# Row normalisation: the first tile's chunks in another partition order, and its last scale on VectorE

## The chip, the cores and the metric

The kernel runs on one core of a Trainium2 chip. The metric is the time of one execution on the device in microseconds, the median of several runs. Three runs of the kernel before took 82.49, 82.53 and 82.61 us, with a median of 82.53 us.

## The reference

The input is a matrix `x` of 1024 rows and 4096 columns in float32. Each row is divided by its Euclidean norm:

```python
norm = np.sqrt(np.sum(x ** 2, axis=-1, keepdims=True) + eps)   # eps = 1e-12
return (x / norm).astype(np.float32)
```

16.78 MB are read and 16.78 MB are written. A row's result depends on that row alone.

## The kernel before

**Tiles.** A tile holds 128 partitions with R = 4 whole rows each, 512 rows or 8.4 MB. There are two tiles (`n_tiles = 1024 / 512`), and each has its own buffer, so neither waits for the other's buffer. Four neighbouring rows are one contiguous run of 4 x 4096 x 4 B = 64 KiB in the input; such a run is called a chunk here. In the view `x_t` (L176) partition p of tile t holds chunk p of that tile, and `out_t` (L177) is the same view of the output.

**Transfers.** All four big transfers are issued from SyncE (SP) and travel on one queue: the load of tile 0, the load of tile 1 (both L192), the store of tile 0, the store of tile 1 (both L213). `first_load_to_front` moves the first load to the very beginning of the program, in front of the start-up barrier. A store is issued when its whole tile has been scaled, and moves the whole tile. `one_barrier_behind_last_store` arranges the end of the program so that it waits for the stores once.

**Calculation, for each tile.** The engines run their instructions in the order of the program, and the order in the loop at L197 to L213 is written by hand. A tile has four row groups, r = 0 to 3: row group r is the r-th row of every partition, 128 x 4096 elements.

- `square_act` (L33): ScalarE squares a row group and accumulates the sum of each row. Groups 0, 1 and 2 go this way.
- `square_dve` (L42): VectorE does the same for group 3, at the start of the tile.
- `norm`: a square root on ScalarE (L53), then a reciprocal on VectorE (L59), each over one number in every partition.
- `scale` (L64): VectorE multiplies a row group in place by its reciprocals. `scale_act` (L69) does the same on ScalarE.

The scales of groups 0, 1 and 3 are on VectorE in both tiles. The last one, of group 2, is on ScalarE in the first tile and on VectorE in the second:

```python
if i < n_tiles - 1:
    g.scale_act(2)
else:
    g.scale(2)
store = nc.sync.dma_start(out=out_t[i], in_=g.flat())
```

Semaphores are placed by the framework from the data that each instruction reads and writes. `Square`, `Sqrt` and the copy with a scale are activation functions of ScalarE. L184 sets the constant eps, and L231 is the program's frame.

Of the kernel before, what the change touches and what calls it, by code (L numbers as in the profile page):

```python
# [8 lines left out]
ACT_F = mybir.ActivationFunctionType  # L9
# [4 lines left out]
class RowGroups:  # L14
# [48 lines left out]
    def scale(self, r):  # L63
        self.nc.vector.tensor_scalar_mul(  # L64
            out=self.x[:, r], in0=self.x[:, r], scalar1=self.rstd[:, r : r + 1]
        )

    def scale_act(self, r):
        self.nc.scalar.activation(  # L69
            out=self.x[:, r],  # L70
            in_=self.x[:, r],
            func=ACT_F.Copy,
            scale=self.rstd[:, r : r + 1],
        )


def first_load_to_front(nc, load):

    def move(program):
        blocks = program.main_func.blocks
        entry = blocks[0].instructions
        if any(i.name == load.name for i in entry):
            return
        body = next(
            b.instructions  # L90
            for b in blocks
            if any(i.name == load.name for i in b.instructions)
        )
        at = next(n for n, i in enumerate(body) if i.name == load.name)
        assert not body[at].sync_info.on_wait
        before = next(
            n
            for n, i in enumerate(entry)
            if i.engine == mybir.EngineType.SP and isinstance(i, mybir.InstDrain)
        )  # L100
        entry.insert(before, body.pop(at))

    nc.at_finalize(move)


def one_barrier_behind_last_store(nc, store):

    SP, POOL = mybir.EngineType.SP, mybir.EngineType.Pool

    def waits(i):
        return i.sync_info.on_wait if i.sync_info is not None else []

    def move(program):
        sem = store.sync_info.on_update[0].id
        tail = program.main_func.blocks[-1].instructions  # L120

        def take(which):
            at = next(n for n, i in enumerate(tail) if which(i))
            return tail.pop(at)

        def place(instructions, which):
            at = max(n for n, i in enumerate(tail) if which(i))
            tail[at:at] = instructions

        arrivals = [  # L130
            n
            for n, i in enumerate(tail)
            if i.engine == SP and isinstance(i, mybir.InstDrain)
        ]
        if any(w.id == sem for w in waits(tail[arrivals[-2]])):
            return
        everything = take(
            lambda i: i.engine == SP and any(w.id == sem for w in waits(i))
        )
        place([everything], lambda i: i.engine == SP and isinstance(i, mybir.InstDrain))  # L140
        reset = take(
            lambda i: i.engine == POOL
            and isinstance(i, mybir.InstDrain)
            and i.is_reset_sema
        )
        clear = take(lambda i: i.engine == POOL and isinstance(i, mybir.InstISA))
        place(
            [reset, clear],
            lambda i: i.engine == POOL and isinstance(i, mybir.InstEventSemaphore),
        )  # L150

    nc.at_finalize(move)


@with_exitstack
def kernel(
    ctx: ExitStack,
    tc: tile.TileContext,
    x: bass.AP,
    axis: bass.AP,  # L160
    eps: bass.AP,
    out: bass.AP,
):
    nc = tc.nc
    P = nc.NUM_PARTITIONS

    assert isinstance(axis, int) and axis in (-1, len(x.shape) - 1)
    eps = float(eps)

    x = x.flatten_outer_dims()  # L170
    out_flat = out.flatten_outer_dims()
    N, D = x.shape
    R = 4
    assert N % (P * R) == 0
    n_tiles = N // (P * R)
    x_t = x.rearrange("(t p r) d -> t p (r d)", p=P, r=R)  # L176
    out_t = out_flat.rearrange("(t p r) d -> t p (r d)", p=P, r=R)  # L177

    io = ctx.enter_context(tc.tile_pool(name="io", bufs=n_tiles))
    scratch_pool = ctx.enter_context(tc.tile_pool(name="scratch", bufs=1))  # L180
    stats = ctx.enter_context(tc.tile_pool(name="stats", bufs=n_tiles))

    eps_t = scratch_pool.tile([P, 1], F32)
    nc.vector.memset(eps_t, eps)  # L184
    sq_act = scratch_pool.tile([P, D], F32)
    sq_dve = scratch_pool.tile([P, D], F32)
    scratch = {"act": sq_act, "dve": sq_dve}

    groups = []
    for i in range(n_tiles):  # L190
        g = RowGroups(nc, io, stats, scratch, D, R, eps_t)
        load = nc.sync.dma_start(out=g.flat(), in_=x_t[i])  # L192
        if i == 0:
            first_load_to_front(nc, load.ins)
        groups.append(g)

    for i, g in enumerate(groups):  # L197
        g.square_dve(R - 1)
        g.square_act(0)
        g.norm(0)  # L200
        g.scale(0)
        g.square_act(1)
        g.norm(1)
        g.norm(R - 1)
        g.scale(1)
        g.scale(R - 1)
        g.square_act(2)
        g.norm(2)
        if i < n_tiles - 1:
            g.scale_act(2)  # L210
        else:
            g.scale(2)
        store = nc.sync.dma_start(out=out_t[i], in_=g.flat())  # L213
    one_barrier_behind_last_store(nc, store.ins)


# [33 lines left out]
```

## Time and profile before

| What | Value |
|---|---|
| median of three runs | 82.53 us |
| the profiled execution: its time | 82.49 us |
| the profiled execution: its span | 80.7 us |
| VectorE busy | 26.2 us (33% of the span) |
| ScalarE busy | 30.1 us (37%) |
| DMA queue: bytes, packets' share of 16 engines | 33.55 MB, 97.0% |
| loads issued (SP) | 0.0 and 0.8 us |
| first instruction on tile 0, on tile 1 | 21.89 us, 41.25 us |
| stores issued (SP) | 39.2 and 56.6 us |
| one scale on VectorE (L64), on ScalarE (L69) | 2.353 us, 3.708 us |

The times in the profile count from the start of the span; what lies between the span and the execution's time is start and end of the program outside it. SPq is the queue of instructions of SyncE, which issues the transfers. In lists of groups and waits, the name left of an arrow waited for the name right of it, and the numbers give the sum, the count and the longest wait. In the chain of waits each line has a start, a length and the work that the later work had to wait for. In a table of stretches each line has a stretch of the span, its length, the busy time of VectorE, ScalarE and GpSimd with the number of their instructions, the clock that TensorE was granted (it does nothing here), the share of the 16 DMA engines that was busy, and the rate in GB/s; a transfer's packet counts where it starts. 512 of the 576 packets carry 64 KiB each, and 64 carry the 4 bytes that tell of a landing.

### The profile page before, as it was taken

The page shows a single profiled execution, that of the slowest core. Times are in us where ns is not written, and L with a number is a line of the kernel's source. Part 1 is how long each engine was busy: PE and PEld are TensorE (multiplying, and loading weights), DVE is VectorE, ACT ScalarE, POOL GpSimd, SP SyncE. Part 2 cuts the span into 40 slices and gives each one's busy share as a digit, 9 for nine tenths or more (in the row PEclk, how much of TensorE's full clock was granted, in tenths as well). Part 3 has the DMA queues.
Part 4 walks back from the last instruction along what each step waited for, and adds up shares of the span by engine and source line. Part 5 has one row for each costly group of instructions (what it writes and reads, how often), then busy time and mean ns, then how long its engine had stood idle before and what let it go on. Part 6 is the DMA issues. An engine that isn't in the chain of part 4 may idle for free.

```text
span 80.7 us, 93 instructions
## 1 busy us (share of the span) xinstructions
DVE 26.2 (33%) x20; ACT 30.1 (37%) x23; POOL 0.2 (0%) x4
## 2 busy tenths in 40 slices
DVE  0000000000199599920059986999000000000000
ACT  6000000000199999989459999930000000000000
POOL 0000000000000000000000000000000000000000
DMA  9099998299998299998399992999993999993990
GB/s 520 0 520 520 520 520 390 130 520 520 520 520 390 130 520 520 520 520 390 130 520 520 520 520 130 390 520 520 520 520 130 390 520 520 520 520 130 390 520 0
DMA packets 576, 33.55 MB, mean 416 GB/s; under 512 B 64, under 2 KB 64, under 8 KB 64
## 3 DMA queue, kind: packets, MB, share of 16 engines
q1 hardware_dynamic: 576, 33.55, 97.0%
HBM read 16.78 MB, written 16.78 MB: 416 GB/s over the span
## 4 chain that ended last, share of the span: by engine, by line
DMA 50%; ACT 10%; DVE 9%; issue 0%
DMA xt<-in_x_dram 50%; ACT sq_act L33 9%; DVE xt L64 9%; ACT rstd L53 1%; DVE rstd L59 0%
## 5 line engine op out<-in xcount | busy, mean ns | idle before, releaser
L33 ACT ACTIVATE sq_act<-xt 128x4096 f32<-128x4096 f32 x6 | 21.6, 3608 | 21.9 <-DMA xt<-in_x_dram 21.9
L42 DVE SCALAR_TENSOR_TENSOR sq_dve<-xt 128x4096 f32<-128x4096 f32 x2 | 8.8, 4425 | 26.8 <-DMA xt<-in_x_dram 26.8
L64 DVE TENSOR_SCALAR xt<-xt,rstd 128x4096 f32<-128x4096 f32 x7 | 16.5, 2353 | 0.2
L69 ACT ACTIVATE xt<-xt,rstd 128x4096 f32<-128x4096 f32 x1 | 3.7, 3708 | 0.2 <-DVE rstd L59 0.2
L53 ACT ACTIVATE rstd<-ssq,eps_t 128x1 f32<-128x1 f32 x8 | 2.1, 288 | 0.1
L59 DVE RECIPROCAL rstd<-rstd 128x1 f32<-128x1 f32 x8 | 1.3, 159 | 2.4 <-ACT rstd L53 2.4
L33 ACT ACT_TABLE_LOAD x1 | 1.3, 1283 | 0.8 <-PEq L231 0.8
L53 ACT ACT_TABLE_LOAD x1 | 1.3, 1283 | 0.0
L33 ACT ACTIVATION_READ_ACCUMULATOR sq_act<-xt 128x1 f32 x6 | 1.1, 185 | 0.0
L184 DVE MEMSET eps_t<- 128x1 f32 x1 | 0.1, 59 | 0.9 <-PEq L231 0.9
L42 DVE DVE_READ_ACCUMULATOR sq_dve<-xt 128x1 f32 x2 | 0.2, 82 | 0.0
L231 POOL MEMSET const-bfloat16-1.0<- 128x1 bf16 x1 | 0.1, 101 | 0.0
L231 POOL MEMSET const-uint8-127<- 128x1 uint8 x1 | 0.1, 101 | 0.0
L231 POOL MEMSET const-float32-0.0<- 128x1 f32 x1 | 0.1, 98 | 0.2 <-issue 0.2
L231 POOL MEMSET const-float32-1.0<- 128x1 f32 x1 | 0.1, 98 | 0.0
## 6 DMA issues: line engine op xcount, KB each, us to landing
xt<-in_x_dram SPq DMA_DIRECT2D x2, 31.2
out_dram<-xt SPq DMA_DIRECT2D x2, 22.6
```

The lines of the kernel that those rows point to most:

```text
L33: self.nc.scalar.activation(out=sq_a, in_=self.x[:, r], func=ACT_F.Square, accum_out=self.ssq[:, r : r + 1],)
L42: self.nc.vector.scalar_tensor_tensor(out=sq_v, in0=self.x[:, r], scalar=1.0, in1=self.x[:, r], op0=ALU.mult, op1=ALU.mult, accum_out=self ...
L53: self.nc.scalar.activation(out=self.rstd[:, r : r + n], in_=self.ssq[:, r : r + n], func=ACT_F.Sqrt, bias=self.eps_t,)
L59: self.nc.vector.reciprocal(out=self.rstd[:, r : r + n], in_=self.rstd[:, r : r + n])
L64: self.nc.vector.tensor_scalar_mul(out=self.x[:, r], in0=self.x[:, r], scalar1=self.rstd[:, r : r + 1])
L69: self.nc.scalar.activation(out=self.x[:, r], in_=self.x[:, r], func=ACT_F.Copy, scale=self.rstd[:, r : r + 1],)
L184: nc.vector.memset(eps_t, eps)
L231: nc = _bacc.Bacc("TRN2", target_bir_lowering=False, num_devices=1)
```

## The change

There are two edits.

1. `scale_act` is removed, and the last scale of the first tile is `scale(2)` on VectorE, as in the second tile.
2. The first tile is loaded and stored through another view. The 128 chunks of the tile are numbered 32b + g, with b = 0 to 3 and g = 0 to 31, and partition 4g + b holds chunk 32b + g. The first partitions of neighbouring groups of four (partitions 0, 4, 8, ...) hold neighbouring chunks 0, 1, 2, ..., and the four partitions of one group hold chunks that are 32 chunks apart, 2 MiB. The second tile keeps the plain view. The view in memory has three dimensions, 32 x 4 x 16384 elements; on chip the tile is 128 x 16384 as before.

```diff
-    def scale_act(self, r):
-        self.nc.scalar.activation(
-            out=self.x[:, r],
-            in_=self.x[:, r],
-            func=ACT_F.Copy,
-            scale=self.rstd[:, r : r + 1],
         )
...
+    B = 4
+    x_f = x.rearrange("(t b g r) d -> t g b (r d)", b=B, g=P // B, r=R)
+    out_f = out_flat.rearrange("(t b g r) d -> t g b (r d)", b=B, g=P // B, r=R)
+    x_v = [x_f[0]] + [x_t[i] for i in range(1, n_tiles)]
+    out_v = [out_f[0]] + [out_t[i] for i in range(1, n_tiles)]
...
-        load = nc.sync.dma_start(out=g.flat(), in_=x_t[i])
+        load = nc.sync.dma_start(out=g.flat(), in_=x_v[i])
...
-        if i < n_tiles - 1:
-            g.scale_act(2)
-        else:
-            g.scale(2)
-        store = nc.sync.dma_start(out=out_t[i], in_=g.flat())
+        g.scale(2)
+        store = nc.sync.dma_start(out=out_v[i], in_=g.flat())
```

More of the change, by code (lines that the diff above doesn't have):

```diff
@@ L65, in scale @@
             out=self.x[:, r], in0=self.x[:, r], scalar1=self.rstd[:, r : r + 1]
-        )
-    def scale_act(self, r):
-        self.nc.scalar.activation(
-            out=self.x[:, r],
-            in_=self.x[:, r],
-            func=ACT_F.Copy,
-            scale=self.rstd[:, r : r + 1],
         )
```

## The prediction

> **What bounds the kernel now.** I read the page first, then the queue's waits, the chain in order of time, the instructions around the first store, and last a table of stretches cut where the transfers change hands.
>
> The page: span, traffic per slice, the one queue.
>
> ```profile
> span 80.7 us, 93 instructions
> DVE 26.2 (33%) x20; ACT 30.1 (37%) x23; POOL 0.2 (0%) x4
> DMA  9099998299998299998399992999993999993990
> DMA packets 576, 33.55 MB, mean 416 GB/s; under 512 B 64, under 2 KB 64, under 8 KB 64
> q1 hardware_dynamic: 576, 33.55, 97.0%
> ```
>
> Both compute engines work a third of the span; the one DMA queue carries 33.55 MB with its packets covering 97.0% of 16 engines' time. The dips in the digits are an artefact: a packet is 64 KiB and counts in the slice where it starts. So the limit is the transfers, in the order load 0, load 1, store 0, store 1.
>
> The queue's own waits, and the chain in order of time (start, length, what):
>
> ```profile
> SPq L245 <- DMA out_dram<-xt: 22.7, 2, 19.3
> SPq L213 <- ACT xt L69: 17.3, 1, 17.3
> ```
>
> ```profile
> 0.79 40.44 DMA xt<-in_x_dram
> 41.23 0.02 issue
> 41.25 3.72 ACT sq_act L33 x2
> ...
> 54.23 2.35 DVE xt L64
> ```
>
> The chain stops at the last calculation, 54.23 + 2.35 = 56.58 us. It doesn't set the end: behind it the program waits 19.3 us in one piece for stores. Store 1 is issued at 56.6 and joins a queue that is busy with store 0 until about 60.4.
>
> The instructions around the first store (start, length, engine, line):
>
> ```profile
> 34.95 0.29 ACT L53 ACTIVATE rstd<-ssq,eps_t 128x1 f32<-128x1 f32 x1
> 35.28 0.16 DVE L59 RECIPROCAL rstd<-rstd 128x1 f32<-128x1 f32 x1 [0.56 <-ACT rstd L53]
> 35.48 3.71 ACT L69 ACTIVATE xt<-xt,rstd 128x4096 f32<-128x4096 f32 x1 [0.23 <-DVE rstd L59]
> 39.21 0.35 SPq L213 DMA_DIRECT2D out_dram<-xt  x1
> 41.25 3.62 ACT L33 ACTIVATE sq_act<-xt 128x4096 f32<-128x4096 f32 x1 [2.06 <-DMA xt<-in_x_dram]
> 41.25 4.43 DVE L42 SCALAR_TENSOR_TENSOR sq_dve<-xt 128x4096 f32<-128x4096 f32 x1 [5.81 <-DMA xt<-in_x_dram]
> ```
>
> Store 0 is issued at 39.21, when ScalarE's 3.71 us scale ends, before load 1 has landed (41.25). VectorE stands idle for 5.81 us there.
>
> The stretches (start:end, length, VectorE, ScalarE, GpSimd busy, clock, DMA share, GB/s):
>
> ```profile
> 1.00:4.05 3.05, 0.00 (x0) 1.07 (x1) 0.00 (x0) 1.00 1.04 344
> 4.05:20.95 16.90, 0.00 (x0) 0.00 (x0) 0.00 (x0) 1.00 1.00 434
> 20.95:40.30 19.35, 11.96 (x9) 16.97 (x12) 0.00 (x0) 1.00 1.00 434
> 40.30:40.52 0.22, 0.00 (x0) 0.00 (x0) 0.00 (x0) 1.00 0.01 0
> 40.52:59.90 19.38, 14.23 (x10) 11.87 (x10) 0.00 (x0) 1.00 1.00 433
> ```
>
> The queue moves 32 rows of 16 packets. In rows 2 to 16 a packet takes 2.418 us by the packet records (65,536 B x 16 / 2.418 us = 434 GB/s, as in the table). The first row alone is slow: 3.16 us in the mean (2.51 to 3.52). Load 0 hands over to load 1, and store 0 to store 1, with no gap. Load 1 hands over to store 0 with a hole: its last packets end between 40.33 and 40.92, and the first store packets begin between 40.53 and 41.02, in the mean 0.18 us later. The row behind the hole takes 2.454 us a packet instead of 2.42.
>
> **The change, part by part.**
>
> *The last scale of tile 0 goes from ScalarE to VectorE.* Removed: one ACT instruction of 3.71 us (L69). Added: one VectorE scale (L64), 2.353 us by the seven in the trace. Both wait for the reciprocal that ends at 35.44. VectorE has nothing else until 41.25, so the added 2.35 us lie in the 5.81 us of idle time and would cost something only if tile 1 landed before 37.8. ScalarE has its next work at 41.25 too, so its 3.71 us bring nothing by themselves. Nothing is queued between this scale and tile 1 on either engine. No table load is involved: the two in the trace belong to L33 and L53, which stay.
>
> What moves is store 0's issue on SP's queue: 39.21 - (3.71 - 2.35) = about 37.85. SP has nothing in front of it, and behind it waits only store 1, at 56.6. The transfer can't begin before load 1 is through its rings at 40.33 to 40.92, so the 1.36 us are not 1.36 us of gain. The question is the 0.18 us hole. Load 0 shows 1.02 us from issue to first packet; store 0's first packet comes 1.32 us after its issue (40.53 - 39.21), hence just as the rings run dry. Issued at 37.85 it would be ready by about 39.2 on the same 1.32 us, at least 1.1 us before the first ring is free. The two handovers whose successor was issued well ahead (0.79 for 21.0, 56.6 for 60.0) show a hole of 0.00. They are the nearest rows, so I take the hole as closing: 0.18 us, and with it the slow row behind it, 2.454 - 2.42 = 0.03. Together -0.21 us. Other end: both of those handovers keep the direction, and this is the only one in which reading HBM turns into writing it; if the hole is the price of turning, the gain is 0.00.
>
> *Tile 0's layout.* The number of packets, their 64 KiB and the 33.55 MB stay, since every partition still holds one contiguous run of four rows. Plainly, partition p holds chunk p. In the new view partition 4g+b holds chunk 32b+g: one partition's step within a group of four is now 32 chunks (2 MiB), and from a group to the next one chunk (64 KiB) instead of four (256 KiB). Load 0 and store 0 use it, 16 of the 32 packet rows. Rows are normalised one by one, so the calculation doesn't see it.
>
> Rows 2 to 8 of load 0 run at 2.418 us with a spread of under 5 ns, the same as load 1; nothing in them varies as memory conflicts would, so I see nothing there that a better order could save. Store 0's rows are at 2.42 to 2.454. Hence 0 for rows 2 to 16. On the upper side the nearest row for a mild loss is the 2.454 us one: 16 x (2.454 - 2.418) = +0.6 us. The farthest is the first row, 3.158: 16 x 0.74 = +11.8 us. I take 0 because 31 of 32 rows are at 2.42 to 2.45 in both directions of transfer.
>
> The Trainium skill, "DMA: Bandwidth & Descriptors", section "Latency and other measured facts", speaks against the change: copies with a row pitch of 2 MiB between partitions ran at 164 GB/s where a padded pitch gave 214. Were that to hold for the 2 MiB step here, an estimate from that page gives 16 rows x 2.418 x (214/164 - 1) = +11.8 us. The page puts it down, as an inference, to partitions streaming in step; this trace has each engine take whole 64 KiB chunks one after the other, so I don't follow the rule.
>
> The first row of load 0 lies wholly on the path: (3.16 - 2.42) = 0.74 us over a later row. Other start addresses might shorten or lengthen it. The best single packet in it took 2.51, which bounds the gain at 3.16 - 2.51 = 0.65. For a loss the worst packet, 3.52, gives 0.36. No row says which, so 0.
>
> *The issue of a transfer with one more dimension.* Load 0's issue stands at the very front, so any growth is on the path. The four plain issues took 0.33 to 0.38 us on SP. Bounds: 0, and one more issue, 0.38. All four lie within 0.05 us although directions and tiles differ, so I take 0. Store 0's issue is covered by the 1.1 us worked out above.
>
> **Sum.** The profiled execution took 82.49, its span 80.70 and 1.79 around it, 0.04 under the median. 82.49 - 0.21 + 0.04 = 82.32 against the median of 82.53: -0.25%. About 0.2%, 0.165 us, is what a measurement of this kernel can tell from no change (its three runs lie within 0.12 us), so 82.365 and 82.695 part the cases.
>
> **Rivals.**
>
> *The hole is the turn from reading to writing.* For it: it is the only turn and the only hole, and it is 0.10 to 0.25 us for every ring, early or late. Against it: the timing of the issue fits just as well. Then nothing changes: 82.53.
>
> *The first row gets shorter.* For it: it is the only stretch where load 0 isn't at 434 GB/s, and the addresses asked for first now lie closer together. Against it: a cold start need not depend on addresses. With half of the 0.65 us: 82.32 - 0.33 = 82.0; with all of it, 81.67.
>
> *Slower: tile 0's packets no longer keep 2.42 us, in load 0 and in store 0.* Place: the 16 rows that use the new view. It decides from a mean growth of (0.21 + 0.165) / 16 = 23 ns a packet, 1%: little beside the 36 ns that the row behind the hole shows. For it: nothing in the profile runs with such a view, and the queue is full, so every nanosecond counts sixteenfold and no cover exists. Against it: the steadiness of the rows. At 36 ns: 82.32 + 0.6 = 82.9. At the first row's rate: 82.32 + 11.8 = 94. The Trainium skill, "SBUF — State Buffer", section "Door 1: The DMA port swizzle (why `[64,N]` ≈ `[32,N]`)", has groups of four partitions share a port; if the new view made the engines take the groups in an order that meets on ports, half the rate is an estimate from that section. No run here shows it.
>
> **How the numbers follow.** Hole closes, layout costs nothing: 0.38, time 82.32, its own range 82.2 to 82.45. Turn: 0.20. Shorter first row: 0.14. Slower packets: 0.28, of which 0.12 is the mild kind and 0.16 the other, anywhere up to tens of us. The range reaches from 81.8 (most of the first row's gain) to 82.95 (the mild loss) and leaves out the 0.16 and some 0.03 below. Faster by over 0.2%: 0.31 of the first case and 0.13 of the third, 0.44. Slower: the whole last case and 0.02 of the turn, where the issue grows, 0.30. The rest, 0.26, is within 0.2%.
>
> **What would show it.** Right: store 0 issued near 37.85, VectorE with eight scales, store packets from about 40.33 with no empty stretch, load 0 landing at 21.9 and load 1 at 41.25, the span near 80.5. The turn: issue at 37.85 but still a stretch with no packet near 40.4. First row: everything behind it shifted to the left, load 0's landing under 21.9. Slower: load 0 landing later than 21.9, and the GB/s of 4.05:20.95 under 434. The prediction falls most easily on the layout, of which the trace holds no instance.

## The result, and the profile after

The changed kernel takes 83.06 us (82.96 to 83.14), the kernel before 82.53 us; the ratio is 1.0061 (95% interval 1.0047 to 1.0074). The forecast was 82.32 us, faster: the sign is wrong, and the time lies above the range.

The page of the changed kernel, the same parts as were shown of before:

```profile
span 81.2 us, 93 instructions
DVE 28.6 (35%) x21; ACT 26.4 (33%) x22; POOL 0.2 (0%) x4
DMA packets 576, 33.55 MB, mean 413 GB/s; under 512 B 64, under 2 KB 64, under 8 KB 64
q1 hardware_dynamic: 576, 33.55, 96.4%
```

The scale moved from ScalarE to VectorE, and packets and bytes are the same. The queue is still what bounds the kernel. The instructions around the first store:

```profile
36.09 0.16 DVE L59 RECIPROCAL rstd<-rstd 128x1 f32<-128x1 f32 x1 [0.56 <-ACT rstd L53]
36.29 2.35 DVE L64 TENSOR_SCALAR xt<-xt,rstd 128x4096 f32<-128x4096 f32 x1
38.67 0.60 SPq L209 DMA_DIRECT2D out_dram<-xt  x1
42.02 3.62 ACT L33 ACTIVATE sq_act<-xt 128x4096 f32<-128x4096 f32 x1 [5.97 <-DMA xt<-in_x_dram]
```

The scale takes its 2.35 us as forecast, but everything lies 0.8 us later, because tile 0 landed later: the issue comes at 38.67 instead of 37.85. It also takes SP 0.60 us, against 0.35 for a plain one. The two loads' issues, both lines from the list of the tile's instructions (shortest, median and longest of the two in ns, then the first and the last start in us), first before, then after:

```profile
L192 SPq DMA_DIRECT2D xt<-in_x_dram x2: 332/357/382, 0.0 to 0.8; - x2
```

```profile
L191 SPq DMA_DIRECT2D xt<-in_x_dram x2: 364/512/660, 0.0 to 1.3; - x2
```

Load 0 is the longer one in both: 0.38 us before, 0.66 after.

Now the stretches, cut where the first ring begins a new set of rows. Where 16 packets start in a stretch, DMA share times length is the mean time of one of them. First before, then after, and last the row before store 0 alone in the kernel after:

```profile
0.00:1.01 1.01, 0.06 (x1) 0.22 (x1) 0.20 (x4) 1.00 0.00 0
1.01:4.10 3.09, 0.00 (x0) 1.06 (x1) 0.00 (x0) 1.00 1.02 339
4.10:21.01 16.91, 0.00 (x0) 0.00 (x0) 0.00 (x0) 1.00 1.00 434
37.90:40.52 2.62, 0.00 (x0) 1.28 (x1) 0.00 (x0) 1.00 0.92 400
40.52:59.95 19.43, 14.23 (x10) 11.87 (x10) 0.00 (x0) 1.00 1.00 432
```

```profile
0.00:1.44 1.44, 0.06 (x1) 0.13 (x1) 0.20 (x4) 1.00 0.00 0
1.44:4.28 2.84, 0.00 (x0) 1.15 (x1) 0.00 (x0) 1.00 1.15 369
4.28:21.20 16.92, 0.00 (x0) 0.00 (x0) 0.00 (x0) 1.00 1.00 434
21.20:40.54 19.34, 14.31 (x10) 13.26 (x11) 0.00 (x0) 1.00 1.00 434
40.54:59.86 19.32, 14.23 (x10) 11.87 (x10) 0.00 (x0) 1.00 1.00 434
```

```profile
38.11:40.54 2.43, 0.53 (x1) 0.00 (x0) 0.00 (x0) 1.00 1.00 432
```

Three things are to be seen. No packet starts before 1.44 us, where the kernel before has its first just after 1.01. The steady rows of load 0 run at 434 GB/s in both views. And the hole is gone: 400 GB/s in the row before store 0 in the kernel before, 432 after; store 0's rows now run at 434 instead of 432.

A ring is the queue's share on one of the 16 DMA engines, and row n is the n-th packet of every ring. By the packet records, the ring that ends last sets the end, so I follow the latest of the 16 at each step. From the end of row 1 on it is one and the same ring. The ring that starts last is another one before and after: its first packet ends at 4.40 and 5.27.

| The latest of the 16 rings | before | after | difference so far |
|---|---|---|---|
| first packet starts | 1.68 | 2.65 | +0.97 |
| row 1 ends | 4.62 | 5.42 | +0.80 |
| row 16, the last of load 1, ends | 40.92 | 41.69 | +0.77 |
| row 17, the first of store 0, starts | 41.02 | 41.69 | +0.67 |
| the last packet ends | 79.80 | 80.34 | +0.54 |

The front lost 0.80 us. Of that, 0.26 came back: 0.03 in the rows of the loads, 0.10 by the hole (that ring's share of it), and 0.13 by the slow row behind it and the slightly slower store rows (2.423 us a packet in rows 18 to 23 before, 2.418 after). The span grew by 0.53.

### The profile page after: what moved, and what is told of

It reads as the page before. It is cut to its first block, busy times and chain, and to the rows that moved or that the text cites. A ratio compares the mean times of both kernels' runs of the same rounds, so it can differ in the third digit from the quotient of the medians.

```text
span 81.2 us, 93 instructions
## 1 busy us (share of the span) xinstructions
DVE 28.6 (35%) x21; ACT 26.4 (33%) x22; POOL 0.2 (0%) x4
## 4 chain that ended last, share of the span: by engine, by line
DMA 50%; ACT 10%; DVE 9%; issue 0%
DMA xt<-in_x_dram 50%; ACT sq_act L33 9%; DVE xt L64 9%; ACT rstd L53 1%; DVE rstd L59 0%
## 5 line engine op out<-in xcount | busy, mean ns | idle before, releaser
L64 DVE TENSOR_SCALAR xt<-xt,rstd 128x4096 f32<-128x4096 f32 x8 | 18.8, 2353 | 0.3
```

Source lines behind the costliest of these rows:

```text
L64: self.nc.vector.tensor_scalar_mul(out=self.x[:, r], in0=self.x[:, r], scalar1=self.rstd[:, r : r + 1])
```

## The experiments

Every kernel was compared with the kernel before on the same chip; its median there was 82.54 us (first and second set) and 82.56 us (third).

**The two parts, one at a time.** The first kernel has only the scale on VectorE:

```diff
-        if i < n_tiles - 1:
-            g.scale_act(2)
-        else:
-            g.scale(2)
+        g.scale(2)
```

> Only the scale moves to VectorE; both tiles keep the plain view. Theory A (the loss comes from the front: load 0's issue with a third dimension fills the last of the 16 rings 0.97 us later, and its first row ends 0.80 us later; the moved scale by itself gains): no hole between load 1 and store 0, first packet at 1.02, the last packet ends some 0.1 to 0.27 us earlier than before, 82.25 to 82.45 us. Theory B (the hole is the turn from reading to writing, and it closed in the changed kernel only because its rings are further apart or because of the new order): a hole of 0.18 us stays, 82.5 us.

Measured: 82.92 us, ratio 1.0050 (1.0033 to 1.0066). Neither theory had this: the scale alone makes the kernel slower. The hole did close. But the last row of load 1 got longer. Its stretch:

```profile
37.84:40.66 2.82, 0.00 (x0) 0.00 (x0) 0.00 (x0) 1.00 1.03 372
```

1.03 x 2.82 = 2.90 us a packet, where the kernel before has 2.42 (0.92 x 2.62). The row behind and all later ones are at 2.418. So the store, queued ahead of time, removed a hole of 0.18 us behind the row and put 0.48 us into it.

The second kernel has only the new view, with the scale left on ScalarE (the second edit of the change without the first).

> Only the new view for the first tile; its last scale stays on ScalarE. Theory A: the third dimension delays store 0's packets after its issue as it delays load 0's (first packet 1.45 us after the issue, last ring 2.65, where the plain load has 1.02 and 1.68). With ScalarE's scale the issue comes at about 40.0 us, so the packets could begin between 41.5 and 42.7, while the rings run dry between 40.55 and 41.7: a hole of about 0.9 us, and 83.06 + 0.9 = about 84.0 us. Theory B (the parts add up: the front costs 0.80 and the hole is always 0.18): 82.53 + 0.8 = 83.3 us.

Measured: 83.30 us, ratio 1.0098 (1.0078 to 1.0118). The time is theory B's, and what I had expected of theory A, a later first packet of the store by the third dimension, didn't occur: issue at 39.97, first store packet at 41.25, 1.28 us, where the plain store before needs 1.32. The mean hole is 0.23 us. The front is as in the changed kernel: first packet at 1.45, row 1 of the last ring ends at 5.37. Hence the new view costs 0.76 us when its store is issued late, and with it the scale on VectorE gains 0.24 us (83.30 to 83.06), while with the plain view it loses 0.38. The parts don't add up; as the next runs show, the difference lies in how the store meets load 1's last row. Note that the banded store isn't ready later: its 16 first packets start 1.48 us after the issue in the mean, those of the plain store before 1.58 us, and in both kernels all 16 rings had run dry and were waiting for it.

Two kernels separate the view of the load from that of the store, with the scale on VectorE. Against the changed kernel, the first has only the first of these edits, the second only the second:

```diff
-        load = nc.sync.dma_start(out=g.flat(), in_=x_v[i])
+        load = nc.sync.dma_start(out=g.flat(), in_=x_t[i])
...
-        store = nc.sync.dma_start(out=out_v[i], in_=g.flat())
+        store = nc.sync.dma_start(out=out_t[i], in_=g.flat())
```

> The scale on VectorE, the first tile loaded in plain order and stored through the new view, so its rows land in other places of the output. Theory A (only the issue at the front costs; the order of addresses costs nothing): store 0's issue takes 0.6 us instead of 0.34 but lies over a second ahead of the rings, so the time is that of the kernel with the scale alone, within 0.1 us. Theory C (the order of addresses costs time in the store's packets): slower than that kernel, by 8 rows times the growth of a packet.

> The scale on VectorE, the first tile loaded through the new view and stored in plain order, so its rows land in other places of the output. Theory A: the whole loss is here; first packet at 1.45, last ring at 2.65, 83.06 us as the changed kernel. Theory C (part of the loss is in the store): between the kernel with the scale alone and 83.06.

Measured: 82.46 us (ratio 0.9991, 0.9977 to 1.0005) with the new view in the store alone, 83.48 us (1.0118, 1.0095 to 1.0140) with it in the load alone. The load's view costs 0.56 us (83.48 against 82.92). Neither theory's bounds hold in either kernel: the store's view was expected to change nothing or to cost, and 83.48 lies above 83.06. The store's view saves 0.4 to 0.5 us in both comparisons (82.46 against 82.92, 83.06 against 83.48), and the load's view costs as much with either store (0.60 us from 82.46 to 83.06). Load 1's last row takes 2.49 us with the banded store and 2.90 without; in the other pair 2.43 and 2.61. The 2.49 is from this stretch, in the profiled execution, which was the fastest of the twelve of its kernel (82.27 us):

```profile
37.76:40.23 2.47, 0.09 (x1) 0.00 (x0) 0.00 (x0) 1.00 1.01 425
```

**Order of addresses, or the moment?** Two theories were left. D: load 1's last row grows because the store's packets are already waiting while it runs, and the new view only makes them ready later after the issue. E: the order of the store's addresses itself prevents the growth. The next pair issues the store 8 us early. In the first tile only three calls are left, and the second tile keeps all of them, indented behind the `else`, with the last scale on VectorE:

```diff
+        if i == 0:
+            g.square_act(0)
+            g.norm(0)
+            g.scale(0)
+        else:
...
```

> Plain views everywhere; in the first tile only row group 0 is squared, normed and scaled, on ScalarE and VectorE, and the rest of that tile's calculation is left out, so that its store is issued at about 30 us, some 10 us before load 1's last packets end. Theory D (the sixteen last packets of load 1 grow because the store's descriptors reach the rings while they run; the earlier they come, the more): a growth of 0.48 us a packet or more in that row, 82.9 us or above. Theory D' (the growth comes only from descriptors being delivered during the last row): the row before or none grows, and the time is that of a store in good time, 82.3 us. Theory E (the growth depends on the order of the store's addresses, not on the moment): about 0.48 us as with the issue at 37.8, 82.9 us.

> The same work left out, the first tile loaded plainly and stored through the new view, so its rows also land in other places; its store is issued at about 30 us as well. Theory D (moment of delivery): the same growth of load 1's last row as with the plain store that early, 82.9 us or whatever that kernel takes. Theory E (order of addresses): a growth of about 0.07 us as with the issue at 37.9, 82.4 us, and 0.4 to 0.5 less than the plain store.

Measured: 83.62 us (ratio 1.0141, 1.0123 to 1.0159) with the plain store, 83.49 us (1.0137, 1.0110 to 1.0163) with the banded one. Load 1's last row in the two:

```profile
37.89:41.43 3.54, 0.00 (x0) 0.00 (x0) 0.00 (x0) 1.00 1.01 296
```

```profile
37.84:41.47 3.63, 0.00 (x0) 0.00 (x0) 0.00 (x0) 1.00 1.02 289
```

3.58 and 3.70 us a packet: the row grows by 1.16 and 1.28 us, whatever the store's view. E falls as an explanation of the whole. D' falls too: only this one row grows (the seven rows of load 1 ahead of it keep 2.418 to 2.428), although the store had been queued for more than three rows. Idle compute engines are not the reason either: in the first of the two no engine calculates from 29.91 to 42.56 us, and the rows ahead of the last stay at 2.42.

Then the moment alone, with the whole calculation and plain views: ScalarE and VectorE share the first tile's last scale, and the share sets the time of the issue: 3328, 3712 or 2048 columns on ScalarE.

```diff
+    def scale_split(self, r, n):
+        self.nc.scalar.activation(
+            out=self.x[:, r, :n],
+            in_=self.x[:, r, :n],
+            func=ACT_F.Copy,
+            scale=self.rstd[:, r : r + 1],
+        )
+        self.nc.vector.tensor_scalar_mul(
+            out=self.x[:, r, n:],
+            in0=self.x[:, r, n:],
+            scalar1=self.rstd[:, r : r + 1],
+        )
...
-            g.scale_act(2)
+            g.scale_split(2, 3328)
```

> Plain views. The first tile's last scale is shared: ScalarE takes 3328 of the 4096 columns (3.71 - 768 x 0.833 ns = 3.07 us), VectorE the rest beside it, so that the store is issued at about 38.55 us, between the 37.82 of the scale on VectorE and the 39.21 of before. Theory D: part of the growth goes and the hole closes too, 82.3 to 82.6 us. Theory E: as with the issue at 37.8, a growth of 0.48 and 82.9 us, until the descriptors come too late and the hole of 0.18 us opens.

> As the kernel with 3328 columns, with 3712 columns on ScalarE (3.39 us), the issue at about 38.87 us. Theory D: the growth of load 1's last row is nearly 0, and the hole smaller than 0.18 us: 82.3 to 82.5 us. Theory E: 82.5 to 82.9 us.

Measured: 82.27 us (ratio 0.9978, 0.9962 to 0.9993) with the issue at 38.56, and 82.21 us (0.9969, 0.9956 to 0.9983) with the issue at 38.81. Both are faster than the kernel before and than the changed one, and a little below theory D's bounds. The second one's issue and the stretch of load 1's last row:

```profile
35.40 3.39 ACT L77 ACTIVATE xt<-xt,rstd 128x3712 f32<-128x3712 f32 x1 [0.23 <-DVE rstd L59]
35.40 0.42 DVE L83 TENSOR_SCALAR xt<-xt,rstd 128x384 f32<-128x384 f32 x1
38.81 0.35 SPq L226 DMA_DIRECT2D out_dram<-xt  x1
```

```profile
37.80:40.24 2.44, 0.00 (x0) 0.99 (x1) 0.00 (x0) 1.00 1.00 430
```

A packet takes 2.43 us and the mean hole is 0.02. An issue 0.4 us later (before) opens the hole; one 1 us earlier (the scale on VectorE) stretches the row.

The third set goes to the early side of that window, with each view, 2048 columns on ScalarE:

> The first tile loaded plainly and stored through the new view (its rows land in other places), its last scale shared half and half between ScalarE and VectorE, so that the store is issued at about 37.45 us. Theory D (only the moment counts, and the new view merely delivers the store's descriptors some 0.4 to 0.6 us later after the issue): load 1's last row grows by 0.2 to 0.5 us a packet, where the issue at 37.88 gave 0.07; 82.6 to 82.9 us. Theory E (the order of the store's addresses protects from the growth in this range): 0.07 as before, 82.45 us.

> Plain views, the last scale of the first tile shared half and half, the store issued at about 37.45 us, earlier than with the scale on VectorE alone (37.82). Theory D: load 1's last row grows by more than the 0.48 us seen there and less than the 1.16 us seen with an issue at 30 us, 82.95 to 83.4 us. If an earlier issue were good: 82.3 us or less.

Measured: 82.89 us (ratio 1.0039, 1.0025 to 1.0054) for the banded store, and 2.77 us a packet in load 1's last row instead of the 2.49 it had with an issue 0.3 us later. So the banded store isn't protected either, which is D's side. The row's stretch:

```profile
37.73:40.52 2.79, 0.00 (x0) 0.00 (x0) 0.00 (x0) 1.00 0.99 376
```

The plain one took 83.24 us (1.0081, 1.0066 to 1.0096). Its time is within D's bounds, but not its row: 2.75 us in the profiled execution, under the 2.90 of the later issue. In that execution load 0's rings began further apart (to 1.99 us) and its tile landed late, so that the issue came at 37.94 instead of 37.45; what I wanted to set, the lead over load 1's last row, was not set.

The runs sorted by that lead, each with one profiled execution. "Issue" is the time from the mean start of load 1's last row to the issue of store 0, negative for an issue ahead of it:

| Store's view | issue (us) | load 1's last row, a packet | mean hole behind it |
|---|---|---|---|
| plain | -8.2 | 3.58 | 0.00 |
| plain, three kernels | -0.27, -0.26, -0.23 | 2.90, 2.61, 2.75 | 0.00 |
| plain | +0.44 | 2.43 | 0.00 |
| plain | +0.74 | 2.43 | 0.02 |
| plain (second tile banded, below) | +0.89 | 2.43 | 0.08 |
| plain (before) | +1.02 | 2.42 | 0.18 |
| banded | -8.3 | 3.70 | 0.00 |
| banded | -0.58 | 2.77 | 0.00 |
| banded, two kernels | -0.25, -0.24 | 2.49, 2.49 | 0.00 |
| banded (after) | -0.08 | 2.43 | 0.00 |
| banded (new view only) | +1.16 | 2.42 | 0.23 |

The moment decides whether the row grows and whether a hole opens. It doesn't order the growth finely: three plain stores within 0.04 us of each other gave 2.61 to 2.90. And near the edge the view matters too: at about -0.25 us the banded store gave 2.49, and the kernels' times differ by 0.4 to 0.5 us. D's explanation of that, a store that is ready later, isn't what the run with the new view alone shows (1.48 us against 1.58 from issue to packets). Why the banded store stretches the row less stays open.

**The front.** One kernel has the second tile banded instead of the first, with 3712 columns of the first tile's last scale on ScalarE; the other is the changed kernel with groups of two. Both cuts are shown against the changed kernel's lines:

```diff
-    x_v = [x_f[0]] + [x_t[i] for i in range(1, n_tiles)]
-    out_v = [out_f[0]] + [out_t[i] for i in range(1, n_tiles)]
+    x_v = [x_t[0], x_f[1]]
+    out_v = [out_t[0], out_f[1]]
```

```diff
-    B = 4
+    B = 2
```

> The second tile is loaded and stored through the new view, the first plainly; the last scale of the first tile is shared with 3712 columns on ScalarE, as in the kernel that took 82.21 us. Both issues with a third dimension now lie behind other transfers. Theory A (the new view costs only where its issue is at the front): 82.2 us within 0.1. Theory C (the order of addresses costs in the packets): 16 rows slower than 2.418 us, above 82.4 us.

> The changed kernel with groups of two partitions in place of four: partition 2g+b holds chunk 64b+g, a third dimension again but other addresses. Theory A (the third dimension's issue costs): first packet at 1.41 to 1.45, the last ring at 2.4 to 2.8, 83.0 to 83.1 us as the changed kernel. If the cost hangs on the number of groups or on the addresses: clearly another time of the first packets, or packets above 2.418 us.

Measured: 82.33 us (ratio 0.9962, 0.9948 to 0.9975) with the second tile banded, faster than before, 0.12 us from the same kernel without a banded tile and so just outside theory A's 0.1, and below C's 82.4. The seven full rows of its banded load, and of its banded store, run at 2.418 to 2.421 us a packet:

```profile
21.02:37.93 16.91, 12.38 (x10) 15.55 (x12) 0.00 (x0) 1.00 1.00 434
59.68:76.58 16.90, 0.00 (x0) 0.00 (x0) 0.00 (x0) 1.00 1.00 434
```

So neither the order of addresses nor the third dimension costs anything to speak of where the issue lies behind other transfers. The groups of two took 82.84 us (1.0029, 1.0013 to 1.0045): below the 83.0 to 83.1 expected. Its first packet starts at 1.45 as with groups of four, and its issue takes 0.66 us, but its last ring starts at 2.28 and row 1 ends at 5.07. Its stretches at the front:

```profile
0.00:1.44 1.44, 0.06 (x1) 0.13 (x1) 0.20 (x4) 1.00 0.00 0
1.44:4.32 2.88, 0.00 (x0) 1.15 (x1) 0.00 (x0) 1.00 1.05 364
4.32:21.23 16.91, 0.00 (x0) 0.00 (x0) 0.00 (x0) 1.00 1.00 434
```

The late first packet thus goes with the third dimension in all four kernels that load tile 0 that way (1.41 to 1.45, against 0.99 to 1.03 in all plain ones). When the last ring starts differs: 2.45 to 2.74 with groups of four, 2.28 with two, 1.46 to 1.99 with the plain view. Row 1 ends at 4.89 to 5.00 us in the mean with groups of four, at 4.76 with two, and at 4.23 to 4.38 in the ten kernels with the plain view. In all four kernels other addresses come first as well, so the third dimension and the order of addresses at the very start are not told apart.

## Why the prediction was wrong

**The step that failed first: "The issue of a transfer with one more dimension ... so I take 0".** The bounds given were 0 and 0.38 us. The issue of load 0 itself grew by 0.28 us (0.66 against 0.38), the first packet came 0.43 us later, the last ring's first packet 0.97 us, and the first row ended 0.80 us later. What was wrong is the argument as much as the size: the four plain issues agree because they are the same kind, so they say nothing of another kind; and SP's issue time isn't the whole price: the first packets of the 16 rings start 0.45 us later in the mean (1.67 against 1.22). By the medians the load's view costs 0.56 to 0.76 us: 0.76 in the kernel with the new view alone, 0.56 and 0.60 with the scale on VectorE. Whether the third dimension or the new addresses at the start cost it was not separated.

**The step that was right in the changed kernel and wrong as stated: "I take the hole as closing ... Together -0.21 us."** Before and after, the hole and the slow rows behind it gave back 0.23 us; the sum had counted only the first of the slow rows. That this lies near the forecast is luck. "Issued well ahead" is not free, although the two nearest rows (load to load, store to store) had suggested it. Alone, this step cost +0.38 us instead of -0.21. A plain store issued ahead of a load's last row stretches that row: by 0.2 to 0.5 us when issued 0.25 us ahead of it, by 1.2 us when issued 8 us ahead. The changed kernel escaped by the other edit: its store's new view takes away 0.46 us with the plain load (82.92 to 82.46) and 0.42 with the banded one. The late front had little part in it, since it moved the issue (by 0.79 us, 37.88 to 38.67) and load 1's last row (by 0.63 us in the mean) together. Why the new view does this stays open.

**"Hence 0 for rows 2 to 16" was right.** The steady rows stay at 2.418 us in the new view. The slower rival named the right sign, load 0 landing after 21.9 (its first instruction came at 22.70 instead of 21.89), and the wrong place: its rows 2 to 16 don't grow at all. The rule on a 2 MiB pitch (the Trainium skill, "DMA: Bandwidth & Descriptors", "Latency and other measured facts"), which the page gives for copies between tensors in HBM, is not borne out here: 2.418 us a packet in both views.

**"The first row gets shorter"** did not come: the mean packet of row 1 took 3.23 to 3.26 us in the three kernels with groups of four, 2.99 to 3.21 in the ten with the plain view, and the ring's start moved by more. **"The hole is the turn from reading to writing"** falls: with plain views and an issue at 38.56 us there is no hole.

**The sum** that the runs give for the last ring: 0.80 at the front, less 0.26 at the handover and in the store's rows, +0.54; the span grew by 0.53. The medians say the same in other parts: 0.60 for the load's view (82.46 to 83.06), and -0.08 for the scale on VectorE together with the store's view (82.54 to 82.46, within the noise).

## What to carry to other kernels

When a queue is full from end to end, look at how late its first row ends: there the transfer's view had its price, once, at the very front; behind other transfers the same view cost nothing clear of the noise (82.33 against 82.21 us). Where the queue turned from loads to stores, the issue had a best moment. The two fastest kernels issued their plain store 0.4 and 0.7 us after the mean start of the load's last row; 0.2 to 0.3 us ahead of it stretched that row, and 1.0 us after it left a hole. The changed kernel's banded store, 0.1 us ahead of it, did neither. Where between these the edges lie was not measured. A cost taken from the nearest rows of a trace holds for their kind only: a handover between two loads did not price one from a load to a store.

## What the runs showed of the hardware

- A store queued behind a load on the same rings lengthened the load's last 64 KiB packet from 2.42 to 3.58 us when it was issued 8 us ahead, and the seven rows before it not beyond 2.43 in the mean. Handovers in one direction show nothing of this size (2.42 to 2.45 us). The Trainium skill, "DMA: Bandwidth & Descriptors", section "Rules for kernel authors", says, for overlapping a transfer with compute, to issue it early, since its fixed setup cost is then hidden; the runs here speak against it at this one place: 82.92 us with the issue at 37.82, 82.21 with the issue at 38.81. What inside the engines makes the packet longer was not shown.
- Once a store had been queued in time, its packets and those of the next store took 2.418 us; after the hole of 0.18 us they took 2.42 to 2.45, 0.13 us over the 16 rows. Why was not shown.
- A view of 32 x 4 chunks took SP 0.60 to 0.66 us to issue instead of 0.33 to 0.38. The longer issue didn't make a store's packets later (1.28 us from issue to first packet, 1.32 for the plain one). It stays open why groups of two fill the last ring sooner than groups of four: each is one profiled execution, and the plain view's last ring scatters by 0.5 us too. A third dimension with plain addresses was not tried; the two inner dimensions merge into one.
